# Strassen's seven products in the value and gate projection of seven retention heads, with fixed PSUM banks

## The chip, the cores and the metric

The kernel runs on one core of a Trainium2 chip. The metric is the device time of one execution in microseconds (us), the median of several runs. PE is the matrix engine (TensorE), DVE the vector engine, ACT the scalar engine, POOL the GpSimd engine, SP the queue that issues the loads. PSUM, into which PE writes its sums, has eight banks; one bank holds 128 x 512 sums in fp32.

## The reference

The model is a trunk of two layers over 256 tokens of width 2048. The first layer is gated retention, the second gated pooling; each is `h + layer(rms_norm(h))`, and a last RMS norm follows. The retention layer, in which the change lies:

```python
h = rms_norm(x, g_norm)
q, k, v, z = split(h @ w_in)                 # 2048 | 2048 | 4096 | 4096 columns
q, k = rope(q), rope(k) * 256 ** -0.5        # 8 heads of 256
o = chunkwise_retention(q, k, v)             # 8 heads, v is 512 wide in each
o = (o - mean(o)) * rsqrt(var(o) + EPS) * gn # per head
return (o * silu(z)) @ w_out                 # 4096 -> 2048
```

So each head has a product of 256 tokens x 2048 with 2048 x 512 for its values, and one of the same size for its gate.

## The kernel before

Everything is fp32, and each fp32 product is made of three products in the format fp32r: an operand is split into a high part (rounded to fp32r) and a low part (what is left), and high x high, high x low and low x high are added in one PSUM bank. The split of a weight is a CAST on ACT (`split`, L94) and a subtraction on DVE (L95).

Weights come from HBM in units of 1 MB (`load`, L104: 128 partitions x 2048 numbers, three buffers with the tag `raw`), all issued by SP in the order of use. A plain unit is split in two halves of 128 x 1024 (`weights`, `pair_of`), and a pair of high and low halves lies in one of five buffers with the tag `w`. So ACT and DVE can be two and a half plain units ahead of PE.

The retention layer loops over eight heads (L272). A head has sixteen units of PE work in this order: four of q and k (`stationary`: 16 blocks of a 512-column and a 256-column matmul each), four of values and four of gate. A block here is 128 of the 2048 rows of the weight, so values and gate have 16 blocks each. `row_products` (L260) makes, for one unit of four blocks, 4 blocks x 2 halves of the tokens x 3 = 24 matmuls of 512 columns, into two banks, one for each half of the tokens. Between them lie the small parts of the head: rope on DVE, the scores `sc` (L299, L304), the mask, the eviction of the values to `vt` and `vs` (L324 to L327), the product of scores and values `po` (L341), its variance (L344 to L346), the gate `gz` (L357), the gated output `og` (L358), its transposes `turned` (L365) and their split into `os` (L370). The gate's products follow the `po` products in the program, so PE has the gate's matmuls while the values are evicted.

A scheduler orders the instructions of each engine when the program is built, by its own estimate of the times; on the chip every engine then keeps that order. PSUM banks are taken from a ring of eight in the retention layer (`ring("all", ...)`), and by number in the output projection.

The output projection `way_out` (L404) already has Strassen's form in part. It makes 256 x 4096 times 4096 x 1024 twice (p = 0 and 1); in each p there are sixteen units by `ORDER` (L29), twelve plain ones ("C") and four ("S") in which a 2 x 2 block product is made with seven block products. An S unit has 7 x 3 = 21 matmuls instead of 24. It needs two sums of weight blocks (`s0`, `s1`, L453 to L456) and four pairs of weight buffers instead of two, and sums of the activations (`forms`), which `sides` (L383) makes once for two S units. The results lie in the banks p1, p5, p6, p7, c11, c21, c12 and c22, and are put together by DVE at the end (L475 to L487). The first layer's `way_out` has its `tmp` and `forms` in memory that the retention layer's buffers held before.

In the first head the inverse norm of the tokens, `rs`, is late: its two halves are transposed by PE into the bank `rst` (L254), and DVE copies one column of each into `rsn` (L255).

Of the kernel before, what the change touches and what calls it, by code (L numbers as in the profile page):

```python
# [13 lines left out]
P = 128  # L14
# [18 lines left out]
SUMS = ("p1", "p5", "p6", "c11", "c21", "c12", "c22", "p7")  # L33
# [13 lines left out]
def kernel(  # L47
# [32 lines left out]
    turns = {"all": 0, "acc": 0, "ret": 0}  # L80
# [4 lines left out]
    def ring(kind, name):  # L85

        start, n = {"all": (0, 8), "acc": (0, 3), "ret": (3, 5)}[kind]
        turns[kind] += 1
        return bank(start + (turns[kind] - 1) % n, name)
# [47 lines left out]
    def column_sums(sums):  # L137

        sp = ev.tile([P, 2, S], F32R, tag="sp", name="sp", bufs=1)
        split(sp[:, 0], sp[:, 1], sums)  # L140
        tot = ring("all", "tot")
# [40 lines left out]


# [11 lines left out]
    with tc.tile_pool(name="rt", bufs=1) as rt:  # L195

        cold = ring("all", "cold")
# [7 lines left out]
        accs = [ring("all", "acc") for _ in range(4)]  # L205
# [45 lines left out]
        rst = ring("all", "rst")  # L251
# [8 lines left out]
        def row_products(acc, c, halves):  # L260

            for i, (hi, lo) in enumerate(halves):
                for j in range(2):
                    k = 4 * c + 2 * i + j
                    for t in range(2):
                        ts = slice(t * P, (t + 1) * P)
                        ws = slice(j * 512, (j + 1) * 512)
                        nc.tensor.matmul(acc[t], hs[:, k, 0, ts], hi[:, ws], start=(k == 0), stop=False)  # L268
                        nc.tensor.matmul(acc[t], hs[:, k, 0, ts], lo[:, ws], start=False, stop=False)  # L269
                        nc.tensor.matmul(acc[t], hs[:, k, 1, ts], hi[:, ws], start=False, stop=(k == KT - 1))  # L270

        for h in range(NH):  # L272
# [3 lines left out]
            for c in range(4 if h else 0):  # L276
                blocks = blocks_of(weights(ret_in[unit]))
                unit += 1
                acc = ring("all", "acc")
                stationary(acc, blocks, hs)  # L280
                joined(qk[:, c], acc)
# [13 lines left out]
            sc = ring("all", "sc").rearrange("p (m s) -> p m s", s=S)  # L295
# [19 lines left out]
            accv = [ring("all", "accv") for _ in range(2)]  # L315
            for c in range(4):
                halves = weights(ret_in[unit])
                unit += 1
                row_products(accv, c, halves)
            vs = rt.tile([P, 2, 2, DV], F32R, tag="vs", name="vs")  # L320
            for t in range(2):
                vt = rt.tile([P, DV], F32, tag="vt", name="vt")
                vm = rt.tile([P, 1], F32, tag="vm", name="vm", bufs=2)
                nc.scalar.activation(vt, accv[t], AF.Identity, scale=rsn[:, t : t + 1], accum_out=vm)  # L324
                nc.vector.tensor_scalar(out=vm, in0=vm, scalar1=-1.0 / DV, scalar2=None, op0=ALU.mult)
                nc.scalar.activation(vs[:, t, 0], vt, AF.Identity, bias=vm)
                nc.vector.scalar_tensor_tensor(  # L327
                    out=vs[:, t, 1], in0=vt, scalar=vm, in1=vs[:, t, 0].bitcast(F32), op0=ALU.add, op1=ALU.subtract
# [3 lines left out]
            po = [ring("all", "po") for _ in range(2)]  # L332
# [21 lines left out]
            gz = rt.tile([P, 2, DV], F32, tag="gz", name="gz")  # L354
            og = rt.tile([P, 2, DV], F32, tag="tcos", name="og")
            for t in range(2):
                nc.scalar.activation(gz[:, t], accz[t], AF.Silu, scale=rsn[:, t : t + 1])  # L357
                nc.vector.scalar_tensor_tensor(  # L358
                    out=og[:, t], in0=po[t], scalar=ors[:, t : t + 1], in1=gz[:, t], op0=ALU.mult, op1=ALU.mult
                )  # L360
            for i in range(2):
                turned = ring("all", "turned")
# [8 lines left out]

    class Sum:


        def __init__(self, i, name, n):
            self.tile, self.n, self.done = bank(i, name), n, 0

        def add(self, a_hi, a_lo, w_hi, w_lo):
            for a, w in ((a_hi, w_hi), (a_hi, w_lo), (a_lo, w_hi)):
                nc.tensor.matmul(self.tile, a, w, start=(self.done == 0), stop=(self.done == self.n - 1))  # L380
                self.done += 1

    def sides(A, first, i, tmp, forms):  # L383


        a = tmp[:, : 4 * S].rearrange("p (k s) -> p k s", s=S)
        s = tmp[:, 4 * S : 4 * S + 2 * P].rearrange("p (k s) -> p k s", s=P)
        blocks = A[:, first + 4 * i : first + 4 * i + 4]
        nc.vector.tensor_tensor(out=a, in0=blocks[:, :, 0].bitcast(F32), in1=blocks[:, :, 1].bitcast(F32), op=ALU.add)
        a11, a21, a12, a22 = a[:, :2, :P], a[:, :2, P:], a[:, 2:, :P], a[:, 2:, P:]  # L390

        def put(form, src):
            split(forms[:, 2 * i : 2 * i + 2, form, 0], forms[:, 2 * i : 2 * i + 2, form, 1], src)

        nc.vector.tensor_tensor(out=s, in0=a21, in1=a22, op=ALU.subtract)
        put(0, s)
        nc.vector.tensor_tensor(out=a21, in0=a11, in1=a21, op=ALU.subtract)
        put(2, a21)
        nc.vector.tensor_tensor(out=s, in0=s, in1=a11, op=ALU.subtract)
        put(1, s)  # L400
        nc.vector.tensor_tensor(out=s, in0=s, in1=a12, op=ALU.add)
        put(3, s)

    def way_out(A, src, first, forms, tmp, work, y, after, ends=False):  # L404
# [8 lines left out]
        for p in range(2):  # L413
# [20 lines left out]
            for n, kind in enumerate(ORDER):  # L434
                unit = src[p * len(ORDER) + n]
                if kind == "C":
# [6 lines left out]
                    if p == 0 and n in (1, 3):  # L443
                        sides(A, first, n // 2, tmp, forms)
# [4 lines left out]

                raw = load(unit)  # L450
                b = raw.rearrange("p (m f) -> p m f", m=4)
                s = [work.tile([P, 2, 512], F32, tag=f"s{i}", name=f"s{i}") for i in range(2)]
                nc.vector.tensor_tensor(out=s[0], in0=b[:, 1:3], in1=b[:, None, 0].broadcast_to([P, 2, 512]), op=ALU.add)  # L453
                b_hi, b_lo = pair_of(raw[:, 512:1536], 1024)
                nc.vector.tensor_tensor(out=s[1][:, 0], in0=s[0][:, 0], in1=b[:, 2], op=ALU.add)
                nc.vector.tensor_tensor(out=s[1][:, 1], in0=s[1][:, 0], in1=b[:, 3], op=ALU.add)  # L456
                b21 = pair_of(raw[:, 1536:], 512)
                t_pairs = [pair_of(x.rearrange("p m f -> p (m f)"), 1024) for x in s]

                def cut(pair, i):  # L460
                    return pair[0][:, i * 512 : (i + 1) * 512], pair[1][:, i * 512 : (i + 1) * 512]

                k1, k2 = strassen_blocks(first, strassen)
                s1, s2, s3, s4 = ((forms[:, strassen, m, 0], forms[:, strassen, m, 1]) for m in range(4))
                strassen += 1
                sums["p1"].add(*blk(k1, 0), *cut((b_hi, b_lo), 0))
                sums["c12"].add(*s4, *cut((b_hi, b_lo), 1))
                sums["c11"].add(*blk(k2, 0), *b21)
                sums["p5"].add(*s1, *cut(t_pairs[0], 0))
                sums["p7"].add(*s3, *cut(t_pairs[0], 1))  # L470
                sums["p6"].add(*s2, *cut(t_pairs[1], 0))
                sums["c21"].add(*blk(k2, 1), *cut(t_pairs[1], 1))
# [298 lines left out]
```

## Time and profile before

| what | value |
|---|---|
| median of 3 runs | 1368.71 us (1368.61 to 1368.79) |
| the profiled execution | 1368.63 us |
| its span, first to last instruction | 1366.5 us |
| PE busy in the span | 1356.7 us, 6888 matmuls |
| PE weight loads busy | 1154.8 us |
| DVE busy | 986.7 us |
| ACT busy | 710.2 us |
| mean granted clock of PE | 0.998 of full speed |
| weights and inputs read | 259.39 MB |

The span is what the profiler saw; the execution is 2.13 us longer. An engine's busy time is the union of its instructions; matmuls overlap each other in the records, so a matmul is shown with some 390 ns though the next one starts about 227 ns after it. The chain of waits is the work that ended last, followed back from the end: the time of an engine in it is the time that the kernel would be shorter if that work were gone. In a timeline row the numbers are the start, the duration, then the engine, the line, the operation, what is written and read, and how often; a bracket holds the idle time before and what ended it.

### The profile page before, as it was taken

The numbers are of one execution on the slowest core, as the hardware profiler recorded it, in microseconds if no ns is written. First come the engines' busy times: TensorE is split into PE (matmuls) and PEld (weight loads), VectorE is DVE, ScalarE is ACT, GpSimd is POOL, SyncE is SP. The second block draws the span as 40 slices with busy tenths as digits, with TensorE's granted clock in tenths as the row PEclk, the third lists the DMA queues.
The fourth block names the chain that finished last, engine by engine and source line by source line (L and its number), as shares of the span: only waits on it lengthen the run. The fifth ranks groups of instructions, "written<-read, shape, count | busy, mean of one in ns | idle before, by whom it ended". The sixth has DMA issues, their size and how long they took to land.

```text
span 1366.5 us, 17656 instructions
## 1 busy us (share of the span) xinstructions
PE 1356.7 (99%) x6888; PEld 1154.8 (85%) x6888; DVE 986.7 (72%) x1415; ACT 710.2 (52%) x992; POOL 25.6 (2%) x34
## 2 busy tenths in 40 slices
PE   9999999999999999999999999999999999999997
PEld 8888888888888888888888888888888888888886
DVE  7866666656565666697778867876885896888676
ACT  7555454545455454455555555445545545555444
POOL 0000000000000000000000000000000000000102
PEclk9999999999999999999999999999999999999999
DMA  8555555545555545565456555555555555556552
GB/s 338 209 165 185 185 191 183 192 163 191 177 191 185 184 165 184 190 235 212 159 216 215 181 191 187 186 189 188 192 201 194 185 185 189 188 197 227 185 214 94
DMA packets 38195, 262.63 MB, mean 192 GB/s; under 512 B 4368, under 2 KB 4496, under 8 KB 7392
## 3 DMA queue, kind: packets, MB, share of 16 engines
q1 hardware_dynamic: 36432, 255.41, 53.7%
q0 software_dynamic: 1536, 5.57, 1.1%
q8 instruction: 54, 0.88, 0.2%
q10 hardware_dynamic: 144, 0.52, 0.1%
q14 instruction: 29, 0.24, 0.0%
HBM read 259.39 MB, written 2.10 MB: 191 GB/s over the span
## 4 chain that ended last, share of the span: by engine, by line
PE 99%; DMA 0%; ACT 0%; DVE 0%; DVEq 0%; issue 0%
PE acc L125 29%; PE c L380 22%; PE acc L126 15%; PE accv L270 4%; PE accv L269 4%; PE accz L270 4%; PE accz L268 4%; PE accz L269 4%; PE accv L268 4%; PE p L380 3%; PE po L341 1%; PE acc L228 1%; PE acc L229 1%; PE turned L365 1%; PE sc L299 0%; DMA xin<-in_xT 0%
## 5 line engine op out<-in xcount | busy, mean ns | idle before, releaser
L95 DVE TENSOR_TENSOR w<-raw,w 128x1024 fp32r<-128x1024 f32 x472 | 568.5, 1210 | 224.0 <-ACT w L94 218.3
L94 ACT CAST w<-raw 128x1024 fp32r<-128x1024 f32 x472 | 488.0, 1040 | 323.3 <-PE acc L126 101.4
L125 PE MATMUL acc<-hs,w 128*128 128x512 f32 x1472 | 513.8, 393 | 0.0
L126 PE MATMUL acc<-hs,w 128*128 128x256 f32 x1472 | 413.5, 281 | 0.0
L125 PEld LDWEIGHTS acc<-hs,w 128*128 128x128 f32 x1472 | 275.6, 187 | 61.4
L126 PEld LDWEIGHTS acc<-hs,w 128*128 128x128 f32 x1472 | 278.1, 189 | 0.5
L380 PE MATMUL c<-w,os 128*128 128x512 f32 x624 | 149.4, 391 | 0.0
L380 PE MATMUL c<-w,gs 128*128 128x512 f32 x624 | 147.1, 390 | 0.0
L380 PEld LDWEIGHTS c<-w,gs 128*128 128x128 f32 x624 | 117.0, 188 | 24.8
L380 PEld LDWEIGHTS c<-w,os 128*128 128x128 f32 x624 | 116.6, 188 | 24.8
L134 ACT COPY hl<-acc 128x256 f32<-128x256 f32 x96 | 35.9, 375 | 147.2 <-PE acc L126 146.2
L270 PE MATMUL accv<-w,hs 128*128 128x512 f32 x256 | 100.0, 391 | 0.0
L270 PE MATMUL accz<-w,hs 128*128 128x512 f32 x256 | 99.9, 390 | 0.0
L269 PE MATMUL accv<-w,hs 128*128 128x512 f32 x256 | 99.9, 390 | 0.0
L268 PE MATMUL accz<-w,hs 128*128 128x512 f32 x256 | 99.9, 390 | 0.0
L269 PE MATMUL accz<-w,hs 128*128 128x512 f32 x256 | 99.8, 390 | 0.0
L268 PE MATMUL accv<-w,hs 128*128 128x512 f32 x256 | 99.5, 389 | 0.0
L125 PE MATMUL acc<-ms,w 128*128 128x512 f32 x256 | 89.0, 390 | 0.0
L126 PE MATMUL acc<-ms,w 128*128 128x256 f32 x256 | 72.2, 282 | 0.0
L94 ACT CAST w<-s 128x1024 fp32r<-128x1024 f32 x32 | 33.6, 1051 | 53.6 <-PE c L380 50.5
L270 PEld LDWEIGHTS accz<-w,hs 128*128 128x128 f32 x256 | 48.1, 188 | 10.2
L125 PEld LDWEIGHTS acc<-ms,w 128*128 128x128 f32 x256 | 48.1, 188 | 10.1
(166 smaller groups left out, 1239.4 us busy)
## 6 DMA issues: line engine op xcount, KB each, us to landing
raw<-in_ret_in SPq DMA_DIRECT2D x92, 1024.0 KB, 4.9
raw<-in_pool_in SPq DMA_DIRECT2D x64, 1024.0 KB, 4.9
raw<-in_ret_out SPq DMA_DIRECT2D x32, 1024.0 KB, 4.9
raw<-in_pool_out SPq DMA_DIRECT2D x32, 1024.0 KB, 5.1
raw<-in_pool_grp SPq DMA_DIRECT2D x16, 1024.0 KB, 4.9
xin<-in_ret_in SPq DMA_DIRECT2D x3, 1024.0 KB, 11.4
xn<-in_xN POOLq DMA_DIRECT2D x4, 512.0 KB, 8.3
out<-xn SPq DMA_DIRECT2D x8, 256.0 KB, 2.3
```

The lines of the kernel that those rows point to most:

```text
L94: nc.scalar.copy(hi, src)
L95: nc.vector.tensor_tensor(out=lo, in0=src, in1=hi.bitcast(F32), op=ALU.subtract)
L125: nc.tensor.matmul(acc, hi, moving[:, k], start=(k == 0), stop=False)
L126: nc.tensor.matmul(acc[:, :S], lo, moving[:, k, 0], start=False, stop=(k == n - 1))
L134: nc.scalar.copy(t, acc[:, S:])
L228: nc.tensor.matmul(accs[c], hi[:, b], hs[:, k], start=(k == 0), stop=False)
L229: nc.tensor.matmul(accs[c][:, :S], lo[:, b], hs[:, k, 0], start=False, stop=(k == KT - 1))
L268: nc.tensor.matmul(acc[t], hs[:, k, 0, ts], hi[:, ws], start=(k == 0), stop=False)
L269: nc.tensor.matmul(acc[t], hs[:, k, 0, ts], lo[:, ws], start=False, stop=False)
L270: nc.tensor.matmul(acc[t], hs[:, k, 1, ts], hi[:, ws], start=False, stop=(k == KT - 1))
L341: nc.tensor.matmul(po[t], ss[:, p, queries], vs[:, keys, q], start=first, stop=last)
L380: nc.tensor.matmul(self.tile, a, w, start=(self.done == 0), stop=(self.done == self.n - 1))
```

## The change

In heads 1 to 7 the values and the gate become one product of 1024 columns (the head's 512 of v beside its 512 of z), and its units come in the order "vvvSzSzz": three plain units of values, an S unit, a plain gate unit, an S unit, two plain gate units. The two S units take the blocks 0 to 3 (four of the sixteen) of both v and z through Strassen's seven products, as `way_out` does, with the same code, now in `strassen_unit`. Head 0 keeps plain units, "vvvvzzzz". The `forms` of the blocks 0 to 3 are made once, in head 0, by `sides`; they lie in the last four blocks of `os`, which only head 7 writes. The buffers for the sums of weights are those of rope (`tcos`, `tsin`).

The values and the gate now end together; in program order the eviction of the values, `po` and its variance come after all the units of the head. DVE has new additions: four that put the seven products together after the second S unit, two that add to the values and two that add to the gate. `vt` has two halves instead of one.

The ring of banks is gone: every tile of the retention layer has a bank with a number. q and k use 4 to 7, `sc` 4, `po` 0 and 1, `turned` 2 and 3, `rst` 2, `tot` 3, and the sums of values and gate the banks of `HEAD_BANKS`. In `way_out` the four p sums have the banks 0 to 3 and the four c sums 4 to 7 (before: p 0 to 2 and 7, c 3 to 6), and its second pair of `turned` banks is 2 and 3.

```diff
-SUMS = ("p1", "p5", "p6", "c11", "c21", "c12", "c22", "p7")
+SUMS = ("p1", "p5", "p6", "p7", "c11", "c21", "c12", "c22")
+HEAD_ORDER = ("vvvvzzzz",) + ("vvvSzSzz",) * (NH - 1)
+HEAD_BANKS = {"c11": 0, "c21": 1, "c12": 2, "c22": 3, "p6": 4, "p1": 5, "p5": 6, "p7": 7}
...
+    def strassen_unit(raw, s, blocks, forms, sums):
+        b = raw.rearrange("p (m f) -> p m f", m=4)
+        nc.vector.tensor_tensor(out=s[0], in0=b[:, 1:3], in1=b[:, None, 0].broadcast_to([P, 2, 512]), op=ALU.add)
+        b_hi, b_lo = pair_of(raw[:, 512:1536], 1024)
+        nc.vector.tensor_tensor(out=s[1][:, 0], in0=s[0][:, 0], in1=b[:, 2], op=ALU.add)
+        nc.vector.tensor_tensor(out=s[1][:, 1], in0=s[1][:, 0], in1=b[:, 3], op=ALU.add)
+        b21 = pair_of(raw[:, 1536:], 512)
+        t_pairs = [pair_of(x.rearrange("p m f -> p (m f)"), 1024) for x in s]
...
+        sums["p1"].add(*a11, *cut((b_hi, b_lo), 0))
+        sums["c12"].add(*s4, *cut((b_hi, b_lo), 1))
+        sums["c11"].add(*a12, *b21)
+        sums["p5"].add(*s1, *cut(t_pairs[0], 0))
+        sums["p7"].add(*s3, *cut(t_pairs[0], 1))
+        sums["p6"].add(*s2, *cut(t_pairs[1], 0))
+        sums["c21"].add(*a22, *cut(t_pairs[1], 1))
...
-        accs = [ring("all", "acc") for _ in range(4)]
+        accs = [bank(4 + c, "acc") for c in range(4)]
...
-        rst = ring("all", "rst")
+        rst = bank(2, "rst")
...
-            accv = [ring("all", "accv") for _ in range(2)]
-            for c in range(4):
-                halves = weights(ret_in[unit])
+            for kind in order:
                 unit += 1
-                row_products(accv, c, halves)
+                if kind == "S":
+                    s = [rt.tile([P, 2, 512], F32, tag=tag, name=tag[:2]) for tag in ("tcos", "tsin")]
+                    k1, k2 = strassen_blocks(0, done)
+                    strassen_unit(load(ret_in[unit - 1]), s, (tokens(k1, 0), tokens(k2, 0), tokens(k2, 1)), forms[:, done], sums)
+                    done += 1
+                    if done == strassen:
+                        nc.scalar.copy(vt[:, 0], sums["p1"].tile)
+                        nc.vector.tensor_tensor(out=vt[:, 1], in0=sums["p6"].tile, in1=vt[:, 0], op=ALU.add)
+                        nc.vector.tensor_tensor(out=gz[:, 0], in0=sums["p5"].tile, in1=vt[:, 1], op=ALU.subtract)
+                        nc.vector.tensor_tensor(out=vt[:, 1], in0=sums["p7"].tile, in1=vt[:, 1], op=ALU.add)
+                        nc.vector.tensor_tensor(out=gz[:, 1], in0=sums["p5"].tile, in1=vt[:, 1], op=ALU.subtract)
+                    continue
+                halves = weights(ret_in[unit - 1])
+                for i, (hi, lo) in enumerate(halves):
+                    for j in range(2):
+                        for t in range(2):
+                            ws = slice(j * 512, (j + 1) * 512)
+                            sums[f"c{t + 1}{1 + 'vz'.index(kind)}"].add(*tokens(plain[kind], t), hi[:, ws], lo[:, ws])
+                        plain[kind] += 1
...
+                v, src = vt[:, t], sums[f"c{t + 1}1"].tile
+                if strassen:
+                    nc.vector.tensor_tensor(out=v, in0=src, in1=v, op=ALU.add)
...
-            po = [ring("all", "po") for _ in range(2)]
+            po = [bank(t, "po") for t in range(2)]
...
-            accz = [ring("all", "accz") for _ in range(2)]
-            for c in range(4):
-                halves = weights(ret_in[unit])
-                unit += 1
-                row_products(accz, c, halves)
+            if h == 0:
+                a = rt.tile([P, 4, S], F32, tag="tcos", name="a")
+                x = rt.tile([P, 2, P], F32, tag="tsin", name="x")
+                sides(hs, 0, 0, a, x, forms)
...
+                g, src = gz[:, t], sums[f"c{t + 1}2"].tile
+                if strassen:
+                    nc.vector.tensor_tensor(out=g, in0=src, in1=g, op=ALU.add)
```

## Rows read from the trace of the kernel before

**Rows 1.** The page's first part: busy us (share of the span) and instructions.

```profile
PE 1356.7 (99%) x6888; PEld 1154.8 (85%) x6888; DVE 986.7 (72%) x1415; ACT 710.2 (52%) x992; POOL 25.6 (2%) x34
```

**Rows 2.** PE's waits for other engines: us in total, times, longest us.

```profile
PE cold L199 <- POOL ones_f L189: 1.0, 1, 1.0
PE acc L228 <- ACT w L94: 0.5, 1, 0.5
```

**Rows 3.** Stretches: length, PE, PEld, DVE, ACT, POOL busy; clock, DMA share, GB/s.

```profile
254.90:324.99 70.09, 70.09 (x349) 59.30 (x349) 43.47 (x59) 34.96 (x47) 0.54 (x1) 1.00 0.53 184
1251.07:1336.00 84.93, 84.93 (x373) 69.85 (x373) 63.02 (x65) 42.75 (x50) 6.48 (x4) 1.00 0.56 198
```

**Rows 4.** The chain in order of time: start us, us, what; plain units, then S units.

```profile
1251.07 43.98 PE c L380 x194
1295.05 0.69 PE p L380 x3
1295.73 1.39 PE c L380 x6
1297.12 1.63 PE p L380 x7
...
1306.31 1.16 PE c L380 x5
1307.47 1.64 PE p L380 x7
```

**Rows 5.** Groups by line and form: busy us, mean ns; idle before, by whom.

```profile
L95 DVE TENSOR_TENSOR w<-raw,w 128x1024 fp32r<-128x1024 f32 x456 | 558.0, 1229 | 218.8 <-ACT w L94 213.1
L94 ACT CAST w<-raw 128x1024 fp32r<-128x1024 f32 x456 | 478.0, 1055 | 303.9 <-PE acc L126 101.4 <-PE accv L270 72.2 <-PE c L380 66.4
L453 DVE TENSOR_TENSOR s<-raw 128x1024 f32<-128x1024 f32 x16 | 19.6, 1224 | 12.1 <-DMA raw<-in_pool_out 6.3 <-DMA raw<-in_ret_out 5.8
L95 DVE TENSOR_TENSOR w<-raw,w 128x512 fp32r<-128x512 f32 x16 | 11.0, 688 | 5.2 <-ACT w L94 5.2
L456 DVE TENSOR_TENSOR s<-s,raw 128x512 f32<-128x512 f32 x16 | 11.0, 686 | 0.0
L425 DVE TENSOR_TENSOR xn<-xn,c 128x512 f32<-128x512 f32 x16 | 10.9, 684 | 9.7 <-PE c L380 9.7
```

**Rows 6.** Timeline of the first head, PE: end of the values, transposes of `rs`.

```profile
52.18 0.39 PE L268 MATMUL accz<-w,hs 128*128 128x512 f32 x1
...
56.72 0.27 PE L254 MATMUL rst<-idt,rs 128*128 128x128 f32 x1
...
63.88 0.27 PE L254 MATMUL rst<-idt,rs 128*128 128x128 f32 x1
```

**Rows 7.** The same stretch on DVE: `tot` is read, `rs` ends, its two copies.

```profile
42.34 0.42 DVE L177 TENSOR_SCALAR rs_a<-tot 128x256 f32<-128x256 f32 x1
...
51.89 0.42 DVE L172 SCALAR_TENSOR_TENSOR rs<-rs_t,rs 128x256 f32<-128x256 f32 x1
...
58.82 0.15 DVE L255 COPY rsn<-rst 128x1 f32<-128x1 f32 x1
...
64.19 0.16 DVE L255 COPY rsn<-rst 128x1 f32<-128x1 f32 x1 [0.48 <-PE rst L254]
```

**Rows 8.** Head 7 into the output projection, DVE: `og`, then `sides`.

```profile
568.51 1.43 DVE L358 SCALAR_TENSOR_TENSOR og<-po,ors,gz 128x512 f32<-128x512 f32 x2 [0.45 <-ACT gz L357]
...
575.06 1.22 DVE L389 TENSOR_TENSOR tmp<-os 128x1024 f32<-128x1024 f32 x1 [0.21 <-PE turned L365]
...
583.06 0.42 DVE L95 TENSOR_TENSOR forms<-tmp,forms 128x256 fp32r<-128x256 f32 x1
...
593.46 0.42 DVE L95 TENSOR_TENSOR forms<-tmp,forms 128x256 fp32r<-128x256 f32 x1
```

**Rows 9.** The same place on PE: the first matmuls that read `forms`.

```profile
592.31 1.79 PE L380 MATMUL p<-w,forms 128*128 128x512 f32 x7
...
594.18 0.62 PE L380 MATMUL c<-w,forms 128*128 128x512 f32 x2
```

More of the change, by code (lines that the diff above doesn't have):

```diff
@@ L140, in column_sums @@
         split(sp[:, 0], sp[:, 1], sums)
-        tot = ring("all", "tot")
+        tot = bank(3, "tot")
         nc.tensor.matmul(tot[:, :S], ones, sp[:, 0], start=True, stop=False)
@@ L181, in wide, with __init__, add, sides @@
         return ap[:, None, :].broadcast_to([P, n, S])
+    class Sum:
+        def __init__(self, i, name, n):
+            self.tile, self.n, self.done = bank(i, name), n, 0
+        def add(self, a_hi, a_lo, w_hi, w_lo):
+            for a, w in ((a_hi, w_hi), (a_hi, w_lo), (a_lo, w_hi)):
+                nc.tensor.matmul(self.tile, a, w, start=(self.done == 0), stop=(self.done == self.n - 1))
+                self.done += 1
+    def sides(A, first, i, a, s, forms):
+        blocks = A[:, first + 4 * i : first + 4 * i + 4]
+        nc.vector.tensor_tensor(out=a, in0=blocks[:, :, 0].bitcast(F32), in1=blocks[:, :, 1].bitcast(F32), op=ALU.add)
+        a11, a21, a12, a22 = a[:, :2, :P], a[:, :2, P:], a[:, 2:, :P], a[:, 2:, P:]
+        def put(form, src):
+            split(forms[:, 2 * i : 2 * i + 2, form, 0], forms[:, 2 * i : 2 * i + 2, form, 1], src)
+        nc.vector.tensor_tensor(out=s, in0=a21, in1=a22, op=ALU.subtract)
+        put(0, s)
+        nc.vector.tensor_tensor(out=a21, in0=a11, in1=a21, op=ALU.subtract)
+        put(2, a21)
+        nc.vector.tensor_tensor(out=s, in0=s, in1=a11, op=ALU.subtract)
+        put(1, s)
+        nc.vector.tensor_tensor(out=s, in0=s, in1=a12, op=ALU.add)
+        put(3, s)
@@ L258, with tokens @@
         unit = 4
[L260 to L270, printed above, removed]
+        forms = os[:, VT - 4 :].rearrange("p k a s -> p (k a s)").rearrange("p (i f l t) -> p i f l t", f=4, l=2, t=P)
+        def tokens(k, t):
+            ts = slice(t * P, (t + 1) * P)
+            return hs[:, k, 0, ts], hs[:, k, 1, ts]
         for h in range(NH):
@@ L312 @@
             split(ss[:, 0], ss[:, 1], sm)
-            accv = [ring("all", "accv") for _ in range(2)]
-            for c in range(4):
-                halves = weights(ret_in[unit])
-                unit += 1
-                row_products(accv, c, halves)
+            order = HEAD_ORDER[h]
+            strassen, plain = order.count("S"), {"v": 2 * order.count("S"), "z": 2 * order.count("S")}
+            sums = {}
+            for name, i in HEAD_BANKS.items():
+                n = 3 * strassen * (name != "c22") + 12 * order.count("v") * (name[0] == "c")
+                if n:
+                    sums[name] = Sum(i, name, n)
@@ L370 @@
                     split_scaled(os[:, e, 0], os[:, e, 1], turned[:, j * S : (j + 1) * S], gn[:, e : e + 1])
[L372 to L402, printed above, removed]
     def way_out(A, src, first, forms, tmp, work, y, after, ends=False):
@@ L450, in way_out @@
                 raw = load(unit)
-                b = raw.rearrange("p (m f) -> p m f", m=4)
                 s = [work.tile([P, 2, 512], F32, tag=f"s{i}", name=f"s{i}") for i in range(2)]
[L453 to L461, printed above, removed]
                 k1, k2 = strassen_blocks(first, strassen)
-                s1, s2, s3, s4 = ((forms[:, strassen, m, 0], forms[:, strassen, m, 1]) for m in range(4))
+                strassen_unit(raw, s, (blk(k1, 0), blk(k2, 0), blk(k2, 1)), forms[:, strassen], sums)
                 strassen += 1
[L466 to L472, printed above, removed]
                 if strassen == NS:
@@ L675, in units, with head_units @@
         return np.ascontiguousarray(w).reshape(-1, P, UNIT)
-    def row_units(w):
-        w = w.reshape(-1, 4, P, w.shape[1] // DV, DV).transpose(3, 0, 2, 1, 4)
-        return np.ascontiguousarray(w).reshape(-1, P, UNIT)
+    def head_units(v, z, order):
+        units, j = [], 0
+        plain = {"v": 2 * order.count("S"), "z": 2 * order.count("S")}
+        for kind in order:
+            if kind == "S":
+                k1, k2 = strassen_blocks(0, j)
+                units.append(np.stack([z[k1], v[k1], z[k2], v[k2]]))
+                j += 1
+            else:
+                units.append((v if kind == "v" else z)[plain[kind] : plain[kind] + 4])
+                plain[kind] += 4
+        return np.stack(units).transpose(0, 2, 1, 3).reshape(-1, P, UNIT)
     def mixed_units(w, first):
```

60 lines of the change are left out of this document (36 added, 24 removed).

## The prediction

> **What bounds the kernel now.** I read four views in this order. The page's first part [rows 1]: PE is busy 1356.7 of 1366.5 us, the next engine, DVE, 986.7. The waits [rows 2]: PE has two in the whole span, 1.5 us together, both at the start; nothing else stops it for another engine. The stretches [rows 3]: between two like points of neighbouring heads lie 70.09 us, PE fills all of them at full clock, DVE 43.47 and ACT 34.96 of them; a stretch of the second output projection is as full, though its DVE is busy 63.02 of 84.93 us. So the kernel lasts as long as its matmuls, one behind the other. How long one is, is read from the distance of starts and not from the duration in the records. The chain in order of time has it [rows 4]: 194 plain matmuls of 512 columns in 43.98 us, 226.7 ns each. The last view, groups by form [rows 5], says who waits for whom beside PE: ACT's splits are held back by PE, which has not yet freed a weight buffer, and DVE's by ACT. The splits are ahead of PE.
>
> So a matmul taken away is worth its slot, as long as the other engines keep PE fed.
>
> **The matmuls.** In each of seven heads two S units of 21 matmuls stand for two plain units of 24; all are 512 columns wide. 48 slots go and 42 come, 42 fewer in seven heads. A plain slot is 226.7 ns. S slots are dearer in the output projection, where three pieces of S units are seen: 3 + 6 + 7 matmuls in 0.69 + 1.39 + 1.63 us, and 5 + 7 in 1.16 + 1.64 [rows 4]; 28 in 6.51 us, 232.5 ns each. Why is not to be seen; the matmuls of these pieces change between many banks and buffers.
> - Out: 48 x 226.7 ns = 10.88 us per head. In: 42 x 232.5 ns = 9.77 us. Difference 1.12 us, in seven heads 7.8 us.
> - Best bound: S slots as cheap as plain ones, 42 x 226.7 ns = 9.5 us. Worst bound: the mixing makes the 144 plain slots of each head's values and gate dearer too, by 5.8 ns; this eats 0.84 us per head, and 2.0 us stay. I take 7.8, since both prices are those of the same code in the same kernel.
>
> [...]
>
> **DVE and ACT, beside PE.** Each S unit adds on DVE one sum of 1024 columns (1.224 us) and two of 512 (0.686 each), and its splits are three of 1.229 and one of 0.688 instead of two of 1.229 [rows 5]: 6.97 us for 2.46, 4.5 more. Eight additions of 128x512 out of PSUM come at the head's end, at 0.684 (the row of `xn`, an addition of the same kind): 5.5 us. DVE rises by 14.5 us per head, from 43.5 to 58.0 of about 69. ACT's casts of 1536 more columns per S unit are 1.6 us (1.055 for 1024 [rows 5]), with a copy for each head: 35.0 to about 39.
>
> What hides them is the lead. Five weight buffers are two and a half plain units, 13.6 us of PE. I followed a head by hand, with v1 starting at 0: v1 to v3 (3 x 24 slots) and `sc` (ten half slots) keep PE until about 17.4 us, S, z, S, z, z until 43.5. DVE is through rope (three passes of 1024 columns and two of 512, 5.0 us by the same rows) and the third value unit's splits at about 9 us; then S1's sums, its splits and the mask (about 1.5 us by its widths) take it to about 17.5, each split on a buffer that PE has freed by then. PE wants the last of them at about 20.9. S2's splits are done at 26.9, wanted from 27.7; the two last gate units' at 28.9 to 32.8, wanted from 32.6 on, half after half. From the second S unit on 2.7 us for putting the seven products together and 3.2 us for the values fall into 10.9 us of PE, with one or two halves of the next head's q. So I cost these at 0; if the lead is gone, an S unit costs 6.97 - 21 x 0.2325 = 2.1 us (the third rival). The output projection bears it out: four S units in 16, DVE 74% busy, PE without a gap [rows 3].
>
> **Loads.** As many units as before, three buffers. A raw buffer of an S unit is held for some 5 us instead of 2.5; DVE waits 12.1 us for loads before the 16 S units of now [rows 5], and PE waits for none. 0, with the same lead as cover.
>
> **Order at the end of a head.** Values and gate end together; the gate's products no longer cover the values' eviction. What takes their place: the values' sums are complete after the second S unit, two gate units (10.9 us) before the head's end, and then come 22 us of the next head's q and k (64 pairs of 512 and 256 columns, one and a half slots each), whose banks 4 to 7 hold only p sums, read before. The next `c11` and `c21` want banks 0 and 1 about 23 us after the gate's end; `po` is then long read. 0.
>
> **Head 0: bank 2.** The gate's `c12` now shares bank 2 with `rst`. Today the gate starts at 52.18, and the transposes into `rst` run at 56.72 and 63.88 [rows 6]; DVE's second copy out of it ends at 64.35 [rows 7]. Now no `c12` product can start before that copy. Its input, `rs`, is complete at 52.31 [rows 7]. In the meantime PE has the products of `c22` (bank 3, shared with `tot`, which DVE has read at 42.76 [rows 7]): five buffers x 6 matmuls = 30 slots, 6.8 us, to 59.0. If the copies stay where they are, PE stands for 64.35 - 58.98 = 5.4 us, once; if the scheduler moves them up right behind `rs`, 0. I take 1.0: the transposes lag behind their inputs by 4.4 and 4.9 us now because PE has queued gate work in front of them, and a PE with nothing else to do would lose most of that lag, but one round of transpose, copy, transpose, copy stays.
>
> [...]
>
> **Head 7 to the output projection.** `og` now waits for the two additions to the gate (1.4 us) and for `po`, which runs about when the gate ends and no longer beside the gate's products: some 5 us later in all, an estimate from those additions and the lag of PE above. `sides` waits for that, as its buffer is `og`'s (its first row waits for `turned`) [rows 8]. Its first forms are ready at 583.5 and read at 592.31, 8.8 us of slack; the last one is ready at 593.88 and read at 594.18, 0.3 us [rows 8, 9]. The last could be late by 5 - 0.3 = 4.7 us; PE has a half unit of plain work (2.7 us) and the other products of the S unit to put before it. 0 to 4.7; I take 0.8. `sides` in head 0 (4.6 us of DVE by 1.22 for its first step [rows 8] and eight of 0.42) falls into a head without S units: 0.
>
> **Sum.** -7.8 + 1.0 + 0.8 = -6.0. The profiled execution took 1368.63 us (span 1366.5 and 2.1 around it), 0.08 below the median shown. 1368.63 - 6.0 = 1362.6 us. Its own range: -9.5 with no stalls is 1359.1; -7.8 with both stalls at half their bounds (5.0) is 1365.8.
>
> **Rivals.**
> 1. All is hidden, banks and forms too: -7.8 to -9.5, 1359.1 to 1360.8. For it: PE shows no wait today at any change of stage. Against it: bank 2. Chance 0.20.
> 2. Little is gained: dear slots throughout (2.0 us stay) or both stalls at their bounds (-7.8 + 5.4 + 4.7 = +2.3): 1366.6 to 1370.9. For it: the trace names no cause for the dear slots, so nothing says that they stop at the S units. Against: the plain units right before the S units of the output projection are cheap [rows 4]. Chance 0.12.
> 3. Slower: DVE becomes the bound in S z S z z. Its work there is 2 x 6.97 + 3 x 2.46 + 2.7 + 3.2 = 27.2 us against 26.1 of PE (2 x 4.88 + 3 x 5.44), so a DVE that comes to S1 without its lead does not catch up there. Lost is 2.1 us in each of 14 S units, 29 us: -7.8 + 29 = +21, 1390; with one S unit in each head, +7, 1375. It decides the sign from 1.1 us of stall per head. What brings it about is the fixed order of DVE's queue: the additions out of PSUM wait for PE's S unit, and behind them in the queue stand the next splits. For it: DVE's share rises to 84%. Against: the lead counted above, and the output projection, where such additions stand among splits without a PE gap. Chance 0.08.
>
> That the seven products don't replace eight can't be: 6 fewer matmuls per head are in the code.
>
> **How the numbers follow.** My case has 0.60. A run can tell a change of about 0.2% from none, 2.7 us. Faster by more than that, below 1366.0: my case and rival 1, and a little of the second's edge: 0.80; within 0.2%: 0.12 from rival 2; slower: 0.08. The range goes from 1358.9, the best bound, to 1367.0, into rival 2.
>
> **What would show it.** PE's count falls by 42 to 6846. The distance from head to head falls from 70.09 to about 69.0 us, with PE as full as before, and DVE about 58 us in it. S slots at 232 ns. In head 0 a gap of PE, or none, between the values' end and the first `c12`. At the first S unit of the output projection a gap of up to some us. Wrong would be: PE waits named L95 or L94 in heads 1 to 7 (rival 3), or no gaps and a distance above 69.7 (dear slots).

## The result and the profile after

The changed kernel takes 1361.88 us (median of 4 runs, 1361.73 to 1362.0); the kernel before took 1368.72 (4 runs) beside it. The ratio is 0.995, with a 95% interval of 0.9933 to 0.9967: 6.8 us less. The forecast was 1362.6 in a range of 1358.9 to 1367.0. The profiled execution took 1361.73 us with a span of 1359.4; the span is 7.1 us shorter than before.

The page's first part, against [rows 1]: 42 matmuls fewer, PE busy 9.1 us less, DVE 86.9 us more. Of PE's 9.1 us, 1.4 are the 26 products at the start (`cold`), which take 4.52 us now and 5.90 before and end ahead of the first real product in both kernels.

```profile
PE 1347.6 (99%) x6846; PEld 1145.6 (84%) x6846; DVE 1073.6 (79%) x1550; ACT 731.6 (54%) x1031; POOL 25.5 (2%) x34
```

PE's waits (us in total, times, longest), against [rows 2]. Two are new: one for `forms`, one for `qs` of head 0. None lies in heads 1 to 7. The first row is at the kernel's start, behind `cold`; the first real product begins at 7.35 us in both kernels, so it costs nothing.

```profile
PE acc L286 <- ACT w L98: 1.9, 1, 1.9
PE cold L257 <- POOL ones_f L247: 1.0, 1, 1.0
PE p L195 <- ACT forms L98: 0.5, 1, 0.5
PE sc L352 <- ACT qs L98: 0.2, 1, 0.2
```

The stretches, against [rows 3]: length, PE, PEld, DVE, ACT and POOL busy, clock, DMA share, GB/s. A head is now 68.89 us from one like point to the next, 1.20 less, still filled by PE at full clock, with 12.0 us more of DVE. The stretch of the second output projection, where the change gives the sums other banks and nothing else, is as long as it was.

```profile
283.10:351.99 68.89, 68.89 (x343) 58.21 (x343) 55.49 (x78) 38.04 (x53) 0.54 (x1) 1.00 0.54 186
1243.95:1328.90 84.95, 84.95 (x374) 69.89 (x373) 63.04 (x65) 42.68 (x50) 6.50 (x4) 1.00 0.57 198
```

The chain in order of time (start us, us, what), against [rows 4]: first an S unit and the plain units of head 1, then an S unit of the second output projection.

```profile
118.90 0.68 PE p L195 x3
119.58 1.36 PE c L195 x6
120.94 1.36 PE p L195 x6
122.30 0.68 PE c L195 x3
122.98 0.68 PE p L195 x3
...
133.40 11.33 PE c L195 x50
...
1288.64 1.39 PE c L195 x6
1290.03 1.63 PE p L195 x7
```

In the heads the S slots are as cheap as plain ones: from the first `p` product on, 21 matmuls take 4.76 us, 226.7 ns each, as against 226.6 for the 50 plain ones further on. In the output projection the same code still takes 3.02 us for 13, 232.3 ns each. It is the same code with seven sums in seven banks in both places, so the change of banks alone does not make a slot dear.

Groups by line and form, DVE, against [rows 5]. The first addition of an S unit in a head (`tc<-raw`) has the duration that the output projection showed, 1.223 us. In the first group DVE still waits 129 us for ACT's casts, less than the 213 before, so its slack shrank and did not vanish.

```profile
L99 DVE TENSOR_TENSOR w<-raw,w 128x1024 fp32r<-128x1024 f32 x442 | 538.7, 1227 | 133.3 <-ACT w L98 129.2
L221 DVE TENSOR_TENSOR tc<-raw 128x1024 f32<-128x1024 f32 x14 | 17.1, 1223 | 0.2
```

Head 0 on PE, against [rows 6]. Both transposes now run within 2 us. Behind the first PE goes on with eight `c` products; behind the second, at 59.11, it has one `sc` product until the next `c` product starts at 59.79.

```profile
57.16 0.27 PE L312 MATMUL rst<-idt,rs 128*128 128x128 f32 x1
57.19 2.09 PE L195 MATMUL c<-w,hs 128*128 128x512 f32 x8
59.11 0.27 PE L312 MATMUL rst<-idt,rs 128*128 128x128 f32 x1
59.55 0.38 PE L352 MATMUL sc<-qs 128*128 128x256 f32 x1 [0.17 <-ACT qs L98]
59.79 5.53 PE L195 MATMUL c<-w,hs 128*128 128x512 f32 x23
```

The same stretch on DVE, against [rows 7]: `rs` is complete at 52.76, the two copies run at 57.60 and 59.59. The second ends at 59.74, 0.05 us before that `c` product. The two rope products, 1.22 us long, start 1.13 us apart: neighbouring DVE instructions overlap by 0.09 us in the records.

```profile
52.33 0.43 DVE L176 SCALAR_TENSOR_TENSOR rs<-rs_t,rs 128x256 f32<-128x256 f32 x1
...
54.60 1.22 DVE L338 TENSOR_TENSOR tcos<-qk,rpr 128x1024 f32<-128x1024 f32 x1
55.73 1.22 DVE L339 TENSOR_TENSOR tsin<-qk,rpr 128x1024 f32<-128x1024 f32 x1
...
57.60 0.15 DVE L313 COPY rsn<-rst 128x1 f32<-128x1 f32 x1
...
59.59 0.15 DVE L313 COPY rsn<-rst 128x1 f32<-128x1 f32 x1
```

Head 7 into the output projection, DVE, against [rows 8]. Seven heads had saved some 7.9 us by then (8.4 less the 0.5 of head 0, below), yet `og` starts 1.3 us and `sides` 1.8 us later than before: against the matmuls around it, `og` is some 9.2 us late.

```profile
569.79 1.41 DVE L446 SCALAR_TENSOR_TENSOR og<-po,ors,gz 128x512 f32<-128x512 f32 x2
...
576.83 1.23 DVE L202 TENSOR_TENSOR tmp<-os 128x1024 f32<-128x1024 f32 x1 [0.27 <-PE turned L453]
...
583.70 0.42 DVE L99 TENSOR_TENSOR forms<-tmp,forms 128x256 fp32r<-128x256 f32 x1
...
593.99 0.42 DVE L99 TENSOR_TENSOR forms<-tmp,forms 128x256 fp32r<-128x256 f32 x1
```

The same place on PE, against [rows 9]: the first product of `forms` starts 8.2 us earlier than before, and the third group of them waits half a microsecond.

```profile
584.11 1.32 PE L195 MATMUL p<-w,forms 128*128 128x512 f32 x5
...
586.77 0.84 PE L195 MATMUL p<-w,forms 128*128 128x512 f32 x2 [0.52 <-ACT forms L98]
```

Where the 7.1 us of span lie is read from like points of both timelines, the first product of head 1 and that of the pooling layer; before, then after:

```profile
77.55 0.39 PE L125 MATMUL acc<-hs,w 128*128 128x512 f32 x1
...
741.80 0.39 PE L125 MATMUL acc<-hs,w 128*128 128x512 f32 x1
```

```profile
78.08 0.39 PE L129 MATMUL acc<-hs,w 128*128 128x512 f32 x1
...
734.70 0.39 PE L129 MATMUL acc<-hs,w 128*128 128x512 f32 x1
```

Head 0 lost 0.5. Seven distances of 1.20 gained 8.4. The pooling layer starts 7.1 earlier: so 0.8 was lost from head 7 to there. From there to the end the difference stays 7.1.

### The profile page after: what moved, and what is told of

Its sections match the earlier page's. It is cut to its first block, busy times and chain, and to the rows that moved or that the text cites. A ratio compares the mean times of both kernels' runs of the same rounds, so it can differ in the third digit from the quotient of the medians.

```text
span 1359.4 us, 17755 instructions
## 1 busy us (share of the span) xinstructions
PE 1347.6 (99%) x6846; PEld 1145.6 (84%) x6846; DVE 1073.6 (79%) x1550; ACT 731.6 (54%) x1031; POOL 25.5 (2%) x34
## 4 chain that ended last, share of the span: by engine, by line
PE 98%; DVE 1%; ACT 0%; DMA 0%; issue 0%; DVEq 0%; SPq 0%; ACTq 0%
PE c L195 43%; PE acc L129 29%; PE acc L130 15%; PE p L195 6%; PE po L427 1%; PE acc L286 1%; PE acc L287 1%; PE turned L453 1%; PE sc L352 0%; DMA xin<-in_ret_in 0%; PE sc L357 0%; ACT w L98 0%; PE turned L562 0%; DVE w L99 0%; DVE tsin L339 0%; DVE tcos L338 0%
## 5 line engine op out<-in xcount | busy, mean ns | idle before, releaser
L99 DVE TENSOR_TENSOR w<-raw,w 128x1024 fp32r<-128x1024 f32 x472 | 558.1, 1192 | 140.7 <-ACT w L98 136.4
L98 ACT CAST w<-raw 128x1024 fp32r<-128x1024 f32 x472 | 479.1, 1026 | 275.5 <-PE c L195 172.8
L195 PE MATMUL c<-w,hs 128*128 128x512 f32 x1284 | 303.9, 390 | 0.0
L195 PEld LDWEIGHTS c<-w,hs 128*128 128x128 f32 x1284 | 239.1, 188 | 49.6
L195 PE MATMUL c<-w,os 128*128 128x512 f32 x666 | 162.6, 392 | 0.0
L99 DVE TENSOR_TENSOR w<-s,w 128x1024 fp32r<-128x1024 f32 x32 | 39.1, 1223 | 24.6 <-ACT w L98 24.5
L129 PEld LDWEIGHTS acc<-ms,w 128*128 128x128 f32 x256 | 48.0, 188 | 10.1
L130 PEld LDWEIGHTS acc<-ms,w 128*128 128x128 f32 x256 | 48.4, 189 | 0.0
L195 PE MATMUL p<-w,os 128*128 128x512 f32 x150 | 40.9, 390 | 0.0
L195 PE MATMUL p<-w,forms 128*128 128x512 f32 x144 | 39.8, 397 | 0.5 <-ACT forms L98 0.5
L195 PEld LDWEIGHTS p<-w,forms 128*128 128x128 f32 x144 | 27.0, 188 | 7.5 <-ACT forms L98 1.0
```

The costliest lines, as they stand in the source:

```text
L98: nc.scalar.copy(hi, src)
L99: nc.vector.tensor_tensor(out=lo, in0=src, in1=hi.bitcast(F32), op=ALU.subtract)
L129: nc.tensor.matmul(acc, hi, moving[:, k], start=(k == 0), stop=False)
L130: nc.tensor.matmul(acc[:, :S], lo, moving[:, k, 0], start=False, stop=(k == n - 1))
```

## The experiments

The theory: the gain is the 42 matmuls a slot each; the losses are bank 2 in head 0 and the late forms. Rivals: the gain is the new order and the banks; or DVE is near its limit and already eats part of the gain.

**Plain units in all heads.** Order and banks stay, the seven products go.

```
-HEAD_ORDER = ("vvvvzzzz",) + ("vvvSzSzz",) * (NH - 1)
+HEAD_ORDER = ("vvvvzzzz",) * NH
...
-                sides(hs, 0, 0, a, x, forms)
```

> The changed kernel with plain units in every head (vvvvzzzz) and without the forms of head 0; the fixed banks, the order of the head's end and everything else stay. Theory: the gain is 42 matmuls and nothing else, and the new banks and order only cost (0.5 us in head 0, 0.8 us at the start of the first output projection by the marks of the two traces). Then the distance from head to head goes back to 70.1 us or a little more (68.89 + 6 x 0.2267 = 70.25), and the time is above the kernel before: 1370 us (1369.5 to 1371.5). Rival: part of the gain comes from the order or the banks (po and the eviction out of the gate's way); then the time stays below the kernel before: 1363 to 1367 us, and the distance below 69.8 us.

Measured: 1370.66 us, ratio 1.0013 (1.0004 to 1.0022). A head of this kernel:

```profile
287.92:357.89 69.97, 69.97 (x349) 59.29 (x347) 43.40 (x60) 34.68 (x48) 0.54 (x1) 1.00 0.54 183
```

Banks and order alone gain 0.12 us per head, and still the kernel is 1.8 us slower than the one before beside it: the two ends lose more than the heads gain (PE waits 1.2 us for split weights in the first S unit of the output projection). From 69.97 to 68.89, 1.08 us per head, is the S units' doing. The gain is the matmuls. Six slots of 226.7 ns would be 1.36, so 0.28 per head is missing.

**The root's transposes in bank 7.**

```
-        rst = bank(2, "rst")
+        rst = bank(7, "rst")
```

> The changed kernel with the transposes of rs in bank 7 instead of bank 2, which the gate's c12 wants. Theory: the 0.53 us that head 0 loses against the kernel before are the wait of c12 for rst: the head ends 0.5 us earlier, 1361.4 us. Rival: they are the price of the slots (the gate's matmuls of one half of the tokens drawn forward, po in one row at the end), or a shift that is lost again at the first output projection: 1361.9 us, no change.

Measured: 1361.3 us (0.9944, 0.9932 to 0.9957), span 1358.9, 0.5 less than the changed kernel's. The transposes lie apart again, with products between them:

```profile
57.28 0.27 PE L312 MATMUL rst<-idt,rs 128*128 128x128 f32 x1
57.31 6.39 PE L195 MATMUL c<-w,hs 128*128 128x512 f32 x27
63.54 0.27 PE L312 MATMUL rst<-idt,rs 128*128 128x128 f32 x1
```

PE's wait for `qs` is gone, and so is its stop behind the second transpose. Head 0's loss was the shared bank.

**`tmp` placed first.** The buffer of `sides` in the output projection gets other memory, to see if the late forms come from its reuse.

```
+        tmp = pl.tile([P, 4 * S + 2 * P + 512], F32, tag="gz", name="tmp")
         xn = pl.tile([P, 2, D], F32, name="xn")
...
-            tmp = pl.tile([P, 4 * S + 2 * P + 512], F32, tag="gz", name="tmp")
```

> The changed kernel with tmp, the work buffer of sides in the first output projection, placed first in its pool, so that it lies over memory of q, k and rope and not over that of og: sides no longer waits for the last transposes of head 7. Theory: the 0.8 us lost at the first output projection come from forms that are late: its 0.5 us wait of PE for forms goes, and 0.5 to 0.8 us with it, 1361.1 to 1361.4 us. Rival: DVE and ACT are full there anyway, or forms lies over late memory too: 1361.9 us.

Measured: 1361.77 us (0.9948, 0.9936 to 0.9961), and the 0.5 us wait for `forms` stays. But `sides` still starts at 576.81 us and still behind `turned`, as in the changed kernel (576.83): the edit did not take away the wait that it was meant to take away. So this run does not show whether the reuse of memory holds `sides` back; that stays open.

**S units side by side.**

```
-HEAD_ORDER = ("vvvvzzzz",) + ("vvvSzSzz",) * (NH - 1)
+HEAD_ORDER = ("vvvvzzzz",) + ("vvvSSzzz",) * (NH - 1)
```

> The changed kernel with the two S units of a head one behind the other (vvvSSzzz). DVE has 13.9 us of work for 9.5 us of PE there. Theory: the lead of five weight buffers still covers it, so no wait of PE; at most the S slots rise from 227 to about 232 ns (42 x 6 ns in 7 heads, 1.8 us): 1361.9 to 1364 us. Rival (DVE as the bound): the lead is used up by the second S unit and PE waits 2 us or more in every head: 1376 us or more.

Measured: 1360.21 us (0.9938, 0.9925 to 0.9952), 1.7 us faster than the changed kernel. A head:

```profile
283.89:352.67 68.78, 68.78 (x342) 58.19 (x341) 55.72 (x78) 38.27 (x53) 0.54 (x1) 1.00 0.54 186
```

Two S units in a row are the harder case for DVE, and no head waits. So DVE is no bound at two S units per head. The values are complete one plain unit earlier, and the wait for `forms` is gone.

**The two edits together.** Order v v v S S z z z and bank 7.

> Both edits that paid alone in one kernel: heads 1 to 7 in the order v v v S S z z z, and the transposed root of head 0 in bank 7. If their gains lie in different places (head 0: 0.5 us; the heads and the start of the output projection: 1.6 us), they add up: 1361.8 - 0.5 - 1.6 = 1359.7 us, and no wait of sc on ACT is left in head 0. If both had only moved one and the same wait, the time stays at 1360.2 us or above.

Measured: 1360.06 us (0.9939, 0.9926 to 0.9951; 1359.87 to 1361.42). No wait for `qs` is left, but against the order alone the median fell by 0.15 and not by 0.5. The shortest spans of the two kernels differ by the expected 0.5 (1357.2 and 1357.7); the two ran on different chips, and these runs don't tell whether the whole 0.5 is to be had. It is the fastest kernel measured here, within the spread of the one before it.

**Four S units in heads 1 to 6.** Eight of sixteen blocks instead of four. Head 7 has the order v v v S S z z z and the root bank 7, as in the kernel of the two edits together; this holds for the other kernels of four S units too.

```
-HEAD_ORDER = ("vvvvzzzz",) + ("vvvSzSzz",) * (NH - 1)
+HEAD_ORDER = ("vvvvzzzz",) + ("vSvSSzSz",) * (NH - 2) + ("vvvSSzzz",)
...
-                sides(hs, 0, 0, a, x, forms)
+                for i in range(2):
...
+                    sides(hs, 0, i, a, x, forms[i], 0)
```

> Heads 1 to 6 take eight of sixteen blocks through the seven products (order v S v S S z S z, two sets of forms, both made in head 0), head 7 stays at v v v S S z z z, root in bank 7. Six heads lose 6 more pairs' worth, 12 - 6 = 6 matmuls each for every two S units: 36 in all, 6 x 1.2 = 7.2 us by the distance that two S units saved a head (1.08 to 1.3 us). Theory of the matmuls: if VectorE still hides, the head distance is 67.5 us and the time 1359.7 - 7.2 = 1352.5 us. The rival that the prediction held for two S units, VectorE as the bound: two S units added 55.5 - 43.5 = 12.0 us of VectorE to a head, four would bring 67.5 us into a distance of 67.5 us, so TensorE waits for weights or sums in every head, the distance is 68.8 us or more, and the time 1360 to 1375 us.

Measured: 1372.69 us (1.0029, 1.0018 to 1.004), slower than before and 12.6 above two S units. A head, then PE's waits over the kernel:

```profile
288.24:359.18 70.94, 69.55 (x337) 56.73 (x335) 62.68 (x88) 40.98 (x57) 0.54 (x1) 1.00 0.53 182
```

```profile
PE c L195 <- ACT w L98: 4.5, 12, 0.5
PE p L195 <- ACT w L98: 1.9, 6, 0.3
```

The rival's outcome, though not by its sum: DVE is busy 62.7 of 70.9 us and not 67.5 (the eight additions out of PSUM come once a head, not once for two S units). But it waits for no other engine between 313.9 and 350.1, from the rope through all S units, and PE's waits for split weights fall into that stretch. PE waits by name for ACT's casts above all, and ACT in its turn waits 47.8 us for DVE's second sum. The limit is local. All PE waits for weights, 7.7 us, are the smaller part of the loss, some 20 us in six heads against the 67.5 expected: matmul records are 0.39 us long and start 0.227 apart, so a stop of less than 0.16 us is not listed. The 48 `p` products of a head start 255 ns apart on average.

**Four in a row.** `"vvSSSSzz"` in heads 1 to 6.

> As the kernel with four S units a head, but in the order v v S S S S z z. VectorE's work of a head is the same (about 67.5 us by the estimate), only its place differs. If what counts is VectorE's sum over a head, the time is that of the other order within 1 us. If what counts is how many S units stand next to each other (each gives TensorE 4.8 us and takes VectorE some 6 us more than a plain unit), this order waits more: 1.5 us or more per head above the other, 9 us in all.

Measured: 1374.96 us (1.0045, 1.0032 to 1.0059), head distance 71.1. 2.3 above the other order: more than the 1 that DVE's sum over a head allowed, much less than the 9 expected if S units next to each other were what counts.

**Four weight buffers instead of five**, in the kernel as changed.

```
-        w = wpool.tile([P, 2, HALF], F32R, tag="w", name="w", bufs=5)
+        w = wpool.tile([P, 2, HALF], F32R, tag="w", name="w", bufs=4)
...
```

> The changed kernel with four buffers for the split weights in place of five; the matmuls and VectorE's work are the same. If the buffers (how far VectorE runs ahead of TensorE) are the cover that hides the S units' additions, the cover gets thinner: the slots beside the S units get dearer or TensorE waits for w, the head distance grows from 68.9 to 69.2 us or more, and the time to 1364 us or more. If the cover was thicker than needed, the distance stays within 0.1 us of 68.9 and the time at 1361.8 us.

Measured: 1362.63 us (0.9959, 0.9944 to 0.9974). A head:

```profile
282.22:350.88 68.66, 68.66 (x342) 58.17 (x341) 55.23 (x78) 37.86 (x52) 0.54 (x1) 1.00 0.54 186
```

In the heads the cover was thicker than needed; the head even became 0.2 us shorter. The seven heads gain some 1.5 us by it, and the kernel still loses 0.75. That is lost at the two ends: PE waits 0.5 us for `qs` in head 0 (0.2 with five buffers) and 0.9 us for `forms` (0.5). So dear slots do not come from a short lead.

**Four S units evenly spread.** `"vSvSzSzS"` in heads 1 to 6.

> Four S units in heads 1 to 6 as before, in the order v S v S z S z S: a plain unit ahead of each. VectorE was busy 62.7 of 70.9 us in a head with the order v S v S S z S z, but without a pause for 34 us of it. If the loss comes from this crowded stretch (place), the even order brings the head distance from 70.9 to 69 us or less and the time to 1361 us or less; the last S unit's sums are then read later, which may cost up to 2 us a head where the next head's first sums need banks 4 to 7. If VectorE's sum over a head decides, the distance stays at 70.9 us and the time at 1372 to 1373 us.

Measured: 1389.99 us (1.0152, 1.0135 to 1.0169), head distance about 74. Neither theory had this. The chain through a head's rope:

```profile
324.14 0.67 PE turned L455 x6
324.83 1.23 DVE tcos L339
```

`tcos` is the buffer of `og`. With the last S unit at the head's end, `og` and its transposes (`turned`) come so late that the next head's rope waits for them (six such waits, 14.8 us, up to 2.8 each), and with it all of DVE's queue. So this run does not decide between place and sum.

**Two of the three additions on GpSimd.** The order as in the first kernel of four S units; this moves the additions of the output projections' S units too.

```
-        nc.vector.tensor_tensor(out=s[1][:, 0], in0=s[0][:, 0], in1=b[:, 2], op=ALU.add)
-        nc.vector.tensor_tensor(out=s[1][:, 1], in0=s[1][:, 0], in1=b[:, 3], op=ALU.add)
+        nc.gpsimd.tensor_tensor(out=s[1][:, 0], in0=s[0][:, 0], in1=b[:, 2], op=ALU.add)
+        nc.gpsimd.tensor_tensor(out=s[1][:, 1], in0=s[1][:, 0], in1=b[:, 3], op=ALU.add)
```

> The kernel with four S units in the order v S v S S z S z, with the second and third addition of each S unit (128x512, 0.68 us each on VectorE) on GpSimd, which is busy 2% of the span; all S units, head 7's two included. VectorE loses 4 x 1.36 = 5.4 us in a head of 70.9 us; GpSimd took 1.3 us for a product of 128x512 at the end of the kernel, so an S unit gets its last factors some 1.2 us later. If VectorE is what bounds the four S units, the head distance falls from 70.9 to between 67.5 and 69.5 us and the time to 1352 to 1364 us. If it is not VectorE (waits on ACT, banks), or if GpSimd is slower beside a busy VectorE, nothing is gained: 1372 us or more.

Measured: 1403.05 us (1.0252, 1.0236 to 1.0267), slower still. The same moments on POOL and on DVE (start us, us):

```profile
334.73 2.04 POOL L224 TENSOR_TENSOR ts<-tc,raw 128x512 f32<-128x512 f32 x1 [45.62 <-DVE tc L222]
336.84 2.14 POOL L225 TENSOR_TENSOR ts<-ts,raw 128x512 f32<-128x512 f32 x1
...
343.67 2.15 POOL L225 TENSOR_TENSOR ts<-ts,raw 128x512 f32<-128x512 f32 x1
```

```profile
335.60 2.25 DVE L99 TENSOR_TENSOR w<-tc,w 128x1024 fp32r<-128x1024 f32 x1
337.94 2.13 DVE L222 TENSOR_TENSOR tc<-raw 128x1024 f32<-128x1024 f32 x1
340.10 1.23 DVE L99 TENSOR_TENSOR w<-ts,w 128x1024 fp32r<-128x1024 f32 x1
...
344.61 0.28 DVE L362 TENSOR_TENSOR sm<-sc,sm 128x128 f32<-128x128 f32 x1
```

In these rows DVE's operations of 1.22 us take 2.13 and 2.25 beside an addition on POOL, and POOL's additions of 128x512 take 2.04 to 2.15, where an operation of that size at the changed kernel's end takes 1.29, the median of eight (1.26 to 2.53). Alone, at 340.10, DVE is back at 1.23. The row of `sm`, which has one input in PSUM, takes the 0.28 us beside POOL (343.67 to 345.82) that it takes without (0.28 in the first kernel of four S units). Nor is `qs` longer, which starts at 334.40 and has its last 0.9 us beside POOL: 1.22. What sets the long ones apart these runs do not show.

The 30 us over the first kernel of four S units are not all put down by this. The sums come later too: ACT waits up to 6.2 us for the second sum, against 3.0 when DVE makes it. And the clock was lower, 0.988 of full speed over the profiled execution against 0.998: behind PE's waits, of up to 2.5 us, PE's granted clock was 0.50 twice in head 1, once in each of heads 2 to 6 and once in the second output projection, and PE is busy 13.1 us longer (1364.4 against 1351.3) for the same 6810 matmuls. One such stretch in head 3 (length, PE, PEld, DVE, ACT and POOL busy, clock, DMA share, GB/s):

```profile
284.60:287.90 3.30, 3.30 (x9) 2.52 (x9) 3.30 (x3) 2.65 (x4) 3.22 (x2) 0.50 0.39 164
```

What each of the three is worth is not separated. In the even order above, whose clock was 0.994 over the profiled execution, it fell in heads 2, 3 and 6, which are 74.0 to 74.4 us long, and not in heads 4 and 5, 73.7 and 73.8 us long; so there it cost little.

**Both.** Even order and GpSimd.

> Both: order v S v S z S z S and the two additions on GpSimd. If place and sum of VectorE's work both count, it is the fastest of the four-S kernels, with a head distance of 67.5 to 68.5 us and 1352 to 1359 us, under the 1360.1 us of the best kernel with two S units. If GpSimd's later factors or the late reading of the last S unit's sums decide, it is no faster than the better of the two single edits.

Measured: 1404.24 us (1.0259, 1.0244 to 1.0274), no better than the worse of the two.

**Head 7 alone in the order v v v S S z z z**, in the kernel as changed.

```
-HEAD_ORDER = ("vvvvzzzz",) + ("vvvSzSzz",) * (NH - 1)
+HEAD_ORDER = ("vvvvzzzz",) + ("vvvSzSzz",) * (NH - 2) + ("vvvSSzzz",)
```

> The changed kernel with the order v v v S S z z z in head 7 alone; heads 1 to 6 stay at v v v S z S z z. The order v v v S S z z z in all heads gained 1.6 us: 0.1 us of distance in each of six heads, 0.6 us, and the rest, 1.0 us, between head 7 and the pooling layer. If that rest is the handing over of head 7 to the output projection (the forms made from the last head's output come late), head 7 alone brings 1361.9 - 1.0 = 1360.9 us, and the 0.5 us wait of the product p for forms is gone. If the gain came from the six heads (or from the order as a whole), the time stays at 1361.6 to 1361.9 us and the wait for forms remains.

Measured: 1360.82 us (0.9941, 0.9927 to 0.9954), 1.06 less than the changed kernel, with the head distance still 68.89. DVE at the border, then PE:

```profile
572.09 1.22 DVE L202 TENSOR_TENSOR tmp<-os 128x1024 f32<-128x1024 f32 x1
...
583.96 0.42 DVE L99 TENSOR_TENSOR forms<-tmp,forms 128x256 fp32r<-128x256 f32 x1
```

```profile
584.21 1.56 PE L195 MATMUL p<-w,forms 128*128 128x512 f32 x6
```

`sides` starts 4.7 us earlier and PE no longer waits. The loss at the output projection was head 7's late `og`; the other 0.6 us of the side-by-side order are the six heads before it.

## Why the prediction was right, step by step

- **PE is the bound, a matmul is worth its slot.** Right: 6846 matmuls, PE full in every head, and the plain kernel of the same banks and order 1.08 us per head longer.
- **The size of it, -7.8 us.** Measured -8.4: 7.6 by the S units and 0.8 by order and banks, which the prediction had at 0. The term "42 x 232.5 ns" was mis-sized, and another left out. S slots in a head cost 226.7 and not 232.5; that alone would have given -9.5, the best bound. But other slots grew dearer, 0.28 us per head, and brought the sum back near the forecast. The stretch of values and gate is not where: in head 1, 120 matmuls from 117.51 to 144.74 us take 226.9 ns each. The dear slots sit among q and k, whose 64 products of 512 columns take 14.97 us per head against 14.73 with plain units, summed over the distances of their starts. Two errors offset each other here; that the sum came out near the forecast is luck.
- **DVE and ACT hidden by the lead.** Right for two S units per head. DVE measured 55.5 and not 58.0: 18 more instructions per head, each overlapping its neighbour by the 0.09 us above, explain 1.6 of the 2.5; 0.9 is left open. How near the third rival was, four S units show: twice the S units in six heads turn a gain of 6.8 us into a loss of 3.9. Its place was not S z S z z as such but the row from the rope to the last S unit in DVE's fixed queue.
- **Order at the end of a head, 0.** Right for this order. The kernel with an S unit last shows what it hinges on: `og` shares `tcos` with the next head's rope, which the prediction did not count among what is late next.
- **Head 0, bank 2: +1.0.** Measured +0.5, shown by bank 7; the 1.0 was an estimate that no run shows. The scheduler moved the second transpose to 2 us behind the first. Of the round transpose, copy, transpose, copy that the forecast left standing, PE fills the first half with eight `c` products; the second half is the 0.5.
- **Head 7 to the output projection: +0.8.** Measured +0.8, 0.5 of it as a named wait. Its mechanism, a late `og`, was right: with the order turned round in that one head, `sides` came 4.7 us earlier and the kernel gained 1.06 us. The lateness was mis-sized: 9.2 us measured for the 5 assumed. The first forms' slack of 8.8 us and the other products that PE has there took up the rest, so that 0.8 came out as forecast is partly luck. That `sides` waits because its buffer is `og`'s is not shown.

Open: why slots of q and k (and of the S units in the output projection) are dearer than 226.7 ns. Fewer weight buffers made the heads' cheaper, so a short lead is not the reason; the order of the units moves them by a tenth of a microsecond per head. More weight buffers were not tried. The traces show where the dear ones lie: among the products of 512 columns in q and k, those in front of the transposes `turned` start 235 ns apart and those behind them 230, before the change and after it. The late `og` puts the transposes 18.5 us behind the head's first product, where it was 4.5, so more products lie in front. With plain units, and with four weight buffers, those in front take 230 to 231 too, so being in front of the transposes is not by itself the reason.

## What to carry to other kernels

Where PE is full, seven products for eight pay up to one slot per matmul saved (here 1.08 of 1.36 us per head), as long as the additions fit into a queue of DVE that still has pauses at that place; its mean share (79% here, 82% in the kernel that lost) does not tell. Put the last S unit well ahead of the stage's end, so that the sums, and whatever shares their buffers, are not late for the next stage. A bank given to two uses, or a last stage that hands over late, cost half a microsecond to one each here, and both were cheap to undo: with both undone the kernel takes 1360.06 us.

## What was not expected of the hardware

An addition on GpSimd of 128x512 took 2.04 to 2.15 us beside DVE in the rows above, and DVE's operations of 1.22 us up to 2.25, so moving 1.4 us of each S unit off DVE left DVE busy for longer in a head (64.0 and 66.0 us in two neighbouring heads against 62.7). And the matmuls of an S unit cost 226.7 ns each in a head and 232.3 in the output projection, with a clock of 1.00 in both.
